# Hybrid decoder step on one core: filler doses, out-projection weights in a chain, two tiles by halves, maxima 0.75 of a head ahead

## The chip, the core and the metric

The kernel runs on one NeuronCore of a Trainium2 chip. The core has five engines with a queue of instructions each: TensorE (PE, matmuls, with its weight loads as PEld), VectorE (DVE), ScalarE (ACT), GpSimd (POOL) and SyncE (SP), which here does nothing but issue DMA transfers. The metric is the device time of one execution in microseconds, the median of several runs.

## The reference

One step of a decoder layer, on a prompt of 2048 positions and on one new position for each of 8 samples. What matters here is the prompt:

```python
h = rms_norm(x, g_norm)
q, k, v, fz, za, u, gv, zc = split(h @ w_in)             # 1024 -> 3592
q, k = rms_norm(q, g_q), rms_norm(k, g_k)                # 8 heads of 64
c = cumsum(log_sigmoid(fz + b_f))                        # per head, over positions
s[t, r] = q[t] . k[r] / 8 + c[t] - c[r]                  # only r <= t
attn = softmax(s) @ v
mix = tril(w_s) @ rms_norm(gv, g_v) + b_s                # in chunks of 128, 4 groups of 128 channels
y = x + concat(attn * silu(za), u * mix * silu(zc)) @ w_out      # 1024 -> 1024
```

The samples attend to 512 paged past positions as well, and also give their k, v, log f and normalised v rows.

## The kernel before, in words

The program has two phases. In the first, TensorE multiplies tiles of 128 positions, or blocks of 512, with the columns of `w_in`; a factor is split into a high and a low part, so that each product is three matmuls. q, k, v and the gates go to DRAM. For the second half of the positions (blocks `cp` 2 and 3) `za`, `u` and `zc` are not computed there: these products are left as *filler*.

The second phase is attention and out-projection. It goes over 32 *units* `(h, c)`, a head and a block of 512 queries, in the order of `UNITS`, which ends with (6,0), (6,1), (6,2), (7,0), (6,3), (7,1), (7,2), (7,3). In a unit (`values`) one step handles 128 keys: two matmuls into a bank `sc` (of three), an exponential on ACT into one of ten buffers `p`, a sum of these on POOL into `acc` (L1066, L1068), and, eight steps at a time, the products `av` of `p` and values. At the unit's end the result goes through ACT and VectorE (`at`), SP stores it (`aT`), and sums and row factors (`rT`) follow.

Into this stream, the order of TensorE's instructions is written by hand; `Pe.clock` is the program's own count of how much TensorE work has been given. Three things are put between the steps:

- *Maxima.* The exponential needs the maximum of each query's row. `maxima` computes scores in pieces into a bank `tp` (of three), which VectorE reduces (L993, L995); the results (`mrow`) are loaded with the queries of a unit by `load_queries` (tile `q2`). `AHEAD` says by how much of a head the maxima run ahead of the units. Their pieces for a head need the head's keys `k2`, whose loads (`load_head`, L906, and L909 for three rows `kx`) are asked for one by one, `LSTEP` apart, beginning in the second step of the unit (h-1, 0).
- *Filler.* `fill` gives as many of its steps (three matmuls into the bank `fl`) as a dose says: `FILL0` in units with c = 0, `FILL7` in the last three, else `FILL`, times the work of a step or piece. A job's weights `fh`, `fl` are asked for when the job before begins.
- *Work that waits for other engines*, given by `later` after so much of `Pe.clock`; `give` puts it into the engines' queues after the last matmul given. The other engines' queues are in the order that a scheduler found with these bounds; each queue is worked through in turn, and an instruction that waits holds up those behind it.

Out-projection (`out_tiles`) needs the 16 weight blocks `wo_hl` (8 blocks `k` of rows, two halves `f` of columns) and, by tile of 128 positions, `g` (attention and mixing, gated, from DRAM) and `xy`, the residual. A weight block is loaded into one of three buffers `raw` (L1137), cast by ACT and its remainder taken by VectorE (`split`, L268 and L273); an input likewise (`am`). The first tiles' inputs are there once the unit (7,0) has gone through its gate (`gate`, POOL's `gz`). After the last unit, `last_phase` runs what is left of 16 tiles.

Of the kernel before, what the change touches and what calls it, by code (L numbers as in the profile page):

```python
# [33 lines left out]
OQ, OK, OV, OF = 0, 512, 1024, 1536  # L34
OZA, OU, OGV, OZC = 1544, 2056, 2568, 3080
NCP = 2
FILL = 0.46
FILL0 = 0.9
FILL7 = 0.95
FLAG = 7000.0  # L40
WOLAG = 9000.0
WOSTEP = 1500.0
OLAG = 9000.0
GTLAG = 8000.0
STLAG = 5000.0
STLAST = 2500.0
SLAG = 4500.0
# [9 lines left out]
NTP = 3  # L57
NAV = 1
UNITS = [(h, c) for h in range(6) for c in range(4)] + [(6, 0), (6, 1), (6, 2), (7, 0), (6, 3), (7, 1), (7, 2), (7, 3)]
AHEAD = 0.65  # L60
LSTEP = 3000.0
LHEAD = 2500.0
VPARTS = 7
# [4 lines left out]
DGATE = 6000.0  # L68
OAHEAD = 3
KORDER = (4, 5, 6, 7, 0, 1, 2, 3)  # L70
WOENG = ('act',)
OFIRST = 2
PAIRS = (14,)
KSTART = 8
PACE = 800.0
# [11 lines left out]
def hymba_step(ctx, tc, x_prompt, x_sample, cache_k, cache_v, cache_logf, page_table, g_norm, w_in,  # L87
# [62 lines left out]
    def bank(tag, n=512):  # L150
        pool, bufs = pool_of[tag]
        return pool.tile([P, n], F32, tag=tag, bufs=bufs, name=tname(tag))


    class Pe:
# [2 lines left out]
        waiting = []  # L158
        given = 0
        loads, load_at = [], 0.0  # L160
        decode, side, steps = 1e12, 1e12, None
        last = None

# [3 lines left out]
    def later(ns, fn):  # L167
        Pe.given += 1
        Pe.waiting.append((Pe.clock + ns, Pe.given, fn))
        Pe.waiting.sort(key=lambda w_: w_[:2])  # L170

    def give():

        seen, last = len(nc.cur_bb.bb.instructions), Pe.last
        Pe.waiting.pop(0)[2]()
        for i in nc.cur_bb.bb.instructions[seen:] if last is not None else ():
            if i.engine != mybir.EngineType.PE:
                tc.add_manual_dep(i, last.name, mybir.DependencyInfo(mybir.DependencyClass.NoSync,
                                                                     mybir.DependencyReason.DATA), reason="given late")

    def pump(all_=False):
        while Pe.waiting and (all_ or Pe.waiting[0][0] <= Pe.clock):
            give()
        if not all_ and Pe.loads and Pe.clock >= Pe.load_at:
            load_next()
        if not all_ and Pe.clock >= Pe.side:
            m = next(mgen)
            mdone[0] += m
            Pe.side = Pe.clock + PACE if mdone[0] < AHEAD * MT else 1e12
        if not all_ and Pe.clock >= Pe.decode:  # L190
            Pe.decode = Pe.clock + (next(Pe.steps, None) or 1e12)

    def load_next():
        Pe.loads.pop(0)()
        Pe.load_at = Pe.clock + LSTEP

    def mm(out, lhsT, rhs, start, stop, ns):
        Pe.last = nc.tensor.matmul(out, lhsT, rhs, start=start, stop=stop).ins  # L198
        pe(ns)
# [65 lines left out]
    def split(hi, lo, src, eng):  # L265

        if eng == "act":
            nc.scalar.copy(hi, src)  # L268
        elif eng == "dve":
            nc.vector.tensor_copy(hi, src)  # L270
        else:
            nc.gpsimd.tensor_scalar(hi, src, 1.0, 0.0, op0=ALU.mult, op1=ALU.add)
        nc.vector.tensor_tensor(lo, src, hi.bitcast(F32), op=ALU.subtract)  # L273
# [566 lines left out]
    def filler():  # L840
        jobs = [(b, f) for f in range(4) for b in (8 + f, 4 * (f // 2) + f % 2, 4 * (f // 2) + 2 + f % 2)]
        nxt = first.pop()
        mxs = {}
        units = []
        for n, (o, f) in enumerate(jobs):
            units.append(nxt)
            if n + 1 < len(jobs):
                nxt = fill_weights(jobs[n + 1][0])
            if n + 2 >= len(jobs):
                continue  # L850
            unit = units.pop()
            while len(unit) < KT:
                yield -1
            for cp in range(NCP, 4):
                if n % 3 == 0:
                    yield from za_steps(unit, 0, f, cp, "fl")
                elif n % 3 == 1:
                    mxs[cp] = s2(t="mxu")
                    yield from u_steps(unit, 0, f, cp, "fl", mxs[cp])
                else:  # L860
                    yield from zc_steps(unit, 0, f, cp, "fl", mxs.pop(cp))
                yield 0
        while min(len(unit) for unit in units) < KT:
            yield -1
        for cp in range(NCP, 4):
            mx = s2(t="mxu")
            yield from u_steps(units[0], 0, f, cp, "fl", mx)
            yield 0
            yield from zc_steps(units[1], 0, f, cp, "fl", mx)
            if cp == 3:  # L870
                break
            yield 0
            while "all" not in heads.get(NH - 1, {}):
                yield -1
            load_out_weights(0)

    def fillers():
        yield from filler()
        load_out_weights(1)
        yield from out_tiles()  # L880

    fgen = fillers()
    debt, hold = [0.0], [0.0]

# [58 lines left out]

    def load_queries(h, c):
        while (h, c) not in shifted:
            if next(mgen, None) is None:
                give()
            pump()

        t = place("q2")  # L950
        a, cs = h * HD, slice(c * 512, (c + 1) * 512)
        for r in range(2):
            nc.sync.dma_start(t[r * HD:(r + 1) * HD, :512].bitcast(F32), qk_hi[a:a + HD, cs])
        nc.sync.dma_start(t[:HD, 512:].bitcast(F32), qk_lo[a:a + HD, cs])
        nc.sync.dma_start(t[HD + 2:HD + 3, 512:].bitcast(F32), mrow[h:h + 1, cs])
        return t
# [170 lines left out]
    def load_out_weights(f):  # L1127

        tiles = []

        def load(n, k):
            if n % 2 == 0:
                tiles.append(s8(F32R, "wo"))
            t = tiles[-1]
            hi, lo = (t[:, (2 * (n % 2) + r) * 512:(2 * (n % 2) + r + 1) * 512] for r in range(2))
            raw = raw2()
            nc.sync.dma_start(raw, wo[k * P:(k + 1) * P, f * 512:(f + 1) * 512])  # L1137

            def parts():
                split(hi, lo, raw, WOENG[n % len(WOENG)])  # L1140
                wo_hl[k, f] = hi, lo
            later(WOLAG, parts)
        for n, k in enumerate(KORDER):
            later(n * WOSTEP, lambda n=n, k=k: load(n, k))

    def gate(k, c):

# [20 lines left out]
    def out_inputs(i):  # L1168

        g, xy = s4(t="g"), s4(t="xy")  # L1170
        nc.sync.dma_start(g, gm[i].rearrange("p k t -> p (k t)"))
        nc.sync.dma_start(xy, x[i * P:(i + 1) * P])
        got = {}

        def parts():
            am = s8(F32R, "am")
            hi, lo = (am[:, r * D:(r + 1) * D] for r in range(2))
            split(hi, lo, g, "act")
            hi, lo = (t.rearrange("p (k t) -> p k t", k=KT) for t in (hi, lo))
            got.update(hi=hi, lo=lo, xy=xy)  # L1180
        later(OLAG, parts)
        return got

    def out_products(i, hi, lo, xy, tags):
        for f in range(2):
            fs = slice(f * 512, (f + 1) * 512)
            po = bank(tags[f])
            for n, k in enumerate(KORDER):
                wh, wl = wo_hl[k, f]
                mm(po, hi[:, k], wh, n == 0, False, 216)  # L1190
                mm(po, hi[:, k], wl, False, False, 216)
                mm(po, lo[:, k], wh, False, n == KT - 1, 216)
                yield 648
            nc.vector.tensor_tensor(xy[:, fs], xy[:, fs], po, op=ALU.add)  # L1194
            yield 0
            if i == NT - 1:
                nc.scalar.dma_start(y[i * P:(i + 1) * P, fs], xy[:, fs])
        if i < NT - 1:
            nc.scalar.dma_start(y[i * P:(i + 1) * P], xy)

    finished = [0]
# [2 lines left out]
    def prepare(i):  # L1204
        if i < NT and i not in ins and finished[0] > i // 4:
            ins[i] = out_inputs(i)
# [3 lines left out]
    def out_tiles():  # L1210

        gs = None
        for i in range(NT):
            while i not in ins or not ins[i] or len(wo_hl) < 2 * KT:
                prepare(i)
                if last_phase[0]:
                    give()
                else:
                    yield -1
            for n in range(1, OAHEAD + 1):  # L1220
                prepare(i + n)
            if i == 8:
                for _ in Pe.steps:
                    pass
                while decoded[0] < B:
                    give()
                gs = decode_out()
            if gs is not None and i < 12:
                next(gs, None)
            yield from out_products(i, **ins.pop(i), tags=("sc", "sc") if last_phase[0] else ("fl", "fl"))  # L1230

    mgen = all_maxima()
    mdone = [0.0]
# [185 lines left out]
```

## Time and profile before

| | us |
|---|---|
| median of 3 runs | 1329.95 |
| lowest, highest | 1324.32, 1331.84 |
| profiled execution: its time | 1327.27 |
| its span, first to last instruction | 1325.5 |
| start of unit (0,0) | 589.3 |
| start of unit (6,0), (6,2), (6,3) | 1010.5, 1029.0, 1066.0 |

The profile is of one execution. Its page gives busy time and share by engine, the span in 40 slices, and the costliest groups of instructions. A group's row reads: line, engine, operation, tiles written and read, shapes, count; then busy time, mean ns of one; then idle time of the engine before them and what ended it. Rows of a timeline read: start, length, engine, line, operation, count, and in brackets the idle time before and what ended it. A stretch's row gives busy time and record count of each engine, TensorE's granted clock (1.00 is full), DMA share and GB/s. A matmul record is one instruction of the hardware; the products `av` are two records each.

### The profile page before, as it was taken

Reading aid. Unit: us, or ns where it says so; the run is one execution under the profiler, and the core shown is the slowest. Engines: PE = TensorE matmul, PEld = TensorE weight load, DVE = VectorE, ACT = ScalarE, POOL = GpSimd, SP = SyncE. Lnnn points to the kernel's source line nnn. Section 1 sums busy time; section 2 is a strip of 40 time slices with the busy share of each in tenths; the row PEclk is TensorE's granted clock in tenths of the full one; section 3 lists DMA queues with packets and bytes.
Section 4 is the critical chain, followed back from the end, with each engine's and each line's share of the span. In section 5 each row is a group of like instructions: output and inputs, shape, how many; then the busy total and the mean of one; then the engine's idle time right before and its main releaser. Section 6 shows DMA issues by size and latency. Waiting matters only on the chain.

```text
span 1325.5 us, 19295 instructions
## 1 busy us (share of the span) xinstructions
PE 1294.4 (98%) x6544; PEld 1005.0 (76%) x6544; DVE 653.7 (49%) x1217; ACT 432.0 (33%) x781; POOL 559.9 (42%) x587
## 2 busy tenths in 40 slices
PE   6999999999999999999999999999999998999998
PEld 6999999999887877866666666666666564688877
DVE  5446664534678654254476544454455544422321
ACT  5542322222222111124444544344444356200100
POOL 3113343423232456215667565567567468600000
PEclk9999999999999999999999999999999898999999
DMA  7644353555213878946344856766474445573221
GB/s 218 197 122 106 88 144 112 151 144 149 73 43 83 291 240 261 310 112 157 81 129 132 221 137 164 205 175 174 131 204 118 112 131 173 184 265 118 96 81 48
DMA packets 189172, 201.43 MB, mean 152 GB/s; under 512 B 40018, under 2 KB 138642, under 8 KB 189050
## 3 DMA queue, kind: packets, MB, share of 16 engines
q1 hardware_dynamic: 185186, 191.43, 50.4%
q10 hardware_dynamic: 3488, 8.39, 1.7%
q8 instruction: 52, 0.85, 0.3%
q14 instruction: 46, 0.38, 0.1%
q0 software_dynamic: 400, 0.38, 0.1%
HBM read 127.43 MB, written 72.73 MB: 151 GB/s over the span
## 4 chain that ended last, share of the span: by engine, by line
PE 89%; DVE 3%; DMA 3%; issue 2%; ACT 1%; POOL 1%; SPq 1%; POOLq 0%; DVEq 0%; ACTq 0%
PE acc L198 35%; PE sc L198 23%; PE fl L198 10%; PE av L198 9%; PE tp L198 6%; PE tp L202 4%; PE pm L198 3%; POOL acc L1068 1%; DMA raw<-in_w_out_dram 1%; DVE mn L995 1%; DMA xp<-in_x_prompt_dram 0%; DMA wraw<-in_w_in_dram 0%; DVE mn L993 0%; DVE wl L281 0%; ACT p L1059 0%
## 5 line engine op out<-in xcount | busy, mean ns | idle before, releaser
L1068 POOL TENSOR_TENSOR acc<-acc,p 128x512 f32<-128x512 f32 (+3 forms) x256 | 289.4, 1131 | 78.7 <-ACT p L1059 63.1
L1059 ACT ACTIVATE p<-sc,zero 128x512 f32<-128x512 f32 (+1 forms) x320 | 194.0, 625 | 171.0 <-PE sc L198 162.6
L198 PE MATMUL acc<-wh,hh 128*128 128x384 f32 (+2 forms) x640 | 228.7, 357 | 0.8 <-ACT hh L268 0.8
L198 PE MATMUL acc<-wl,hh 128*128 128x384 f32 (+2 forms) x640 | 222.5, 348 | 1.0 <-DVE wl L281 1.0
L198 PE MATMUL acc<-wh,hl 128*128 128x384 f32 (+2 forms) x640 | 222.8, 348 | 0.7 <-DVE hl L273 0.6
L198 PE MATMUL sc<-q,k 128*128 128x512 f32 (+7 forms) x640 | 202.7, 398 | 6.7 <-ACT p L1059 6.6
L198 PE MATMUL sc<-wo,am 128*128 128x512 f32 x720 | 164.1, 390 | 0.0
L198 PEld LDWEIGHTS sc<-wo,am 128*128 128x128 f32 x720 | 134.9, 188 | 28.2
L995 DVE TENSOR_REDUCE mn<-tp 128x1 f32<-128x320 f32 (+5 forms) x192 | 118.9, 632 | 75.5 <-PE tp L198 74.6
L198 PEld LDWEIGHTS sc<-q,k 128*128 128x128 f32 (+1 forms) x640 | 119.1, 197 | 27.1 <-ACT p L1059 11.4
L198 PE MATMUL av<-p,vst 128*64 128x512 f32 (+3 forms) x640 | 137.2, 549 | 0.0
L198 PE MATMUL tp<-k,q 66*128 66x384 f32 (+6 forms) x320 | 122.3, 399 | 8.5 <-DMA k<-kx 1.7
L198 PEld LDWEIGHTS acc<-wh,hh 128*128 128x128 f32 x640 | 120.7, 189 | 8.2 <-ACT hh L268 1.5
L198 PEld LDWEIGHTS acc<-wh,hl 128*128 128x128 f32 x640 | 120.4, 188 | 6.8 <-DVE hl L273 1.6
L198 PEld LDWEIGHTS acc<-wl,hh 128*128 128x128 f32 x640 | 120.8, 189 | 5.9 <-DVE wl L281 1.4
L261 POOL TENSOR_SCALAR sm<-sm 128x6 f32<-128x6 f32 (+3 forms) x84 | 20.3, 242 | 243.4 <-DVE sm L447 169.9
L198 PEld LDWEIGHTS av<-p,vst 128*64 128x64 f32 x640 | 48.8, 139 | 68.2 <-issue 58.6
L993 DVE TENSOR_REDUCE mn<-tp 128x1 f32<-128x512 f32 (+7 forms) x128 | 66.8, 563 | 53.2 <-PE tp L198 52.7
L262 POOL TENSOR_TENSOR sm<-sm,mhalf 128x6 f32<-128x6 f32 (+3 forms) x84 | 89.0, 1060 | 6.7
L198 PEld LDWEIGHTS tp<-k,q 66*128 66x128 f32 x320 | 60.6, 191 | 37.6 <-DVE mn L995 6.2
L1066 POOL TENSOR_TENSOR acc<-p 128x512 f32<-128x512 f32 x32 | 41.1, 1284 | 110.4 <-ACT p L1059 98.9
L1194 DVE TENSOR_TENSOR xy<-xy,sc 128x512 f32<-128x512 f32 x30 | 20.6, 687 | 120.1 <-PE sc L198 120.1
(213 smaller groups left out, 1902.3 us busy)
## 6 DMA issues: line engine op xcount, KB each, us to landing
kb<-in_cache_k_dram SPq DMA_DIRECT2D x32, 256.0 KB
k<-qk_hi SPq DMA_DIRECT2D x32, 256.0 KB
q<-qk_hi SPq DMA_DIRECT2D x64, 128.0 KB
vb<-in_cache_v_dram SPq DMA_DIRECT2D x32, 256.0 KB
g<-gm SPq DMA_DIRECT2D x16, 512.0 KB
xy<-in_x_prompt_dram SPq DMA_DIRECT2D x16, 512.0 KB
out_dram<-xy ACTq DMA_DIRECT2D x15, 512.0 KB
qk_hi<-qkh SPq DMA_DIRECT2D x32, 192.0 KB
```

The lines of the kernel that those rows point to most:

```text
L198: Pe.last = nc.tensor.matmul(out, lhsT, rhs, start=start, stop=stop).ins
L202: Pe.last = nc.tensor.transpose(out, in_, idn).ins
L261: nc.gpsimd.tensor_scalar(r, ss, inv_n, EPS, op0=ALU.mult, op1=ALU.add)
L262: nc.gpsimd.tensor_tensor(r, r, mhalf[:rows, :n], op=ALU.pow)
L993: nc.vector.tensor_reduce(part[:, j_ % 4, n_:n_ + 1], sp, axis=AX.X, op=ALU.min)
L995: nc.vector.tensor_reduce(part[:, j % 4, n:n + 1], sp, axis=AX.X, op=ALU.min)
L1059: nc.scalar.activation(p[:, n0:], sp[:, n0:], AF.Exp, bias=zero1, scale=-1.0)
L1066: nc.gpsimd.tensor_tensor(acc, p0, p, op=ALU.add)
L1068: nc.gpsimd.tensor_tensor(acc[:, n0:], acc[:, n0:], p[:, n0:], op=ALU.add)
L1194: nc.vector.tensor_tensor(xy[:, fs], xy[:, fs], po, op=ALU.add)
```

## The change

It changes numbers and the places where three things are asked for.

1. `AHEAD` goes from 0.65 to 0.75, and maxima drawn by `load_queries` are counted in `mdone`.
2. The doses go from 0.46, 0.9, 0.95 to 0.42, 0.85, 0.6 (`FILL`, `FILL0`, `FILL7`).
3. The filler no longer stops until the last head's loads are all given, and no longer asks for out-projection's weights itself: it puts their half into `wo_due`, and `pump` asks for it once the last head is loaded. Of a half's eight blocks three are asked for at once, and each further one when the cast of the block three before it is given, 8 us of `Pe.clock` after its load instead of 9.
4. Out-projection goes over half tiles: (0, first half), (1, first), (0, second), (1, second), then the others as before. A half tile waits only for its own half of the weights. Inputs of tile 2 are asked for at the half tile before it, those of tiles 3 to 5 at its start.

```diff
-FILL = 0.46
-FILL0 = 0.9
-FILL7 = 0.95
+FILL = 0.42
+FILL0 = 0.85
+FILL7 = 0.6
-WOLAG = 9000.0
+WOLAG = 8000.0
-AHEAD = 0.65
+AHEAD = 0.75
...
         if not all_ and Pe.loads and Pe.clock >= Pe.load_at:
             load_next()
+        if Pe.wanted:
+            Pe.wanted()
...
             yield 0
-            while "all" not in heads.get(NH - 1, {}):
-                yield -1
-            load_out_weights(0)
+            wo_due.append(0)
 
     def fillers():
         yield from filler()
-        load_out_weights(1)
+        wo_due.append(1)
         yield from out_tiles()
 
+    wo_due = []
+
+    def wanted():
+        if wo_due and "all" in heads.get(NH - 1, {}):
+            load_out_weights(wo_due.pop(0))
+    Pe.wanted = wanted
...
         while (h, c) not in shifted:
-            if next(mgen, None) is None:
+            m = next(mgen, None)
+            if m is None:
                 give()
+            else:
+                mdone[0] += m
             pump()
...
             def parts():
-                split(hi, lo, raw, WOENG[n % len(WOENG)])
+                split(hi, lo, raw, "act")
                 wo_hl[k, f] = hi, lo
+                if n + 3 < KT:
+                    load(n + 3, KORDER[n + 3])
             later(WOLAG, parts)
-        for n, k in enumerate(KORDER):
-            later(n * WOSTEP, lambda n=n, k=k: load(n, k))
+        for n in range(3):
+            later(n * WOSTEP, lambda n=n: load(n, KORDER[n]))
...
-        for i in range(NT):
-            while i not in ins or not ins[i] or len(wo_hl) < 2 * KT:
+        halves = [(i, f) for f in range(2) for i in range(NHALF)] + [(i, f) for i in range(NHALF, NT) for f in range(2)]
+        for n, (i, f) in enumerate(halves):
+            while i not in ins or not ins[i] or (KORDER[-1], f) not in wo_hl:
...
-            for n in range(1, OAHEAD + 1):
-                prepare(i + n)
+            for j in range(min(NHALF, n + 2) if n < NHALF else i + 1, n - NHALF + 2 if n < 2 * NHALF else i + OAHEAD + 1):
+                prepare(j)
```

TensorE's instructions number the same on both sides; their order differs from the end of the first phase on. Numbers behind a tile's name tell its uses apart. In unit (6,2) before, TensorE's queue: `tp<-k2,q1` are maxima of head 7, `maskb` their mask.

```order
L198 MATMUL tp_1960_10895<-maskb_91,identb_84 128x128
L198 MATMUL tp_1961_10901<-k2_1897_10642,q1_999_6032 128x512
L198 MATMUL tp_1962_10904<-k2_1897_10642,q1_999_6032 128x512
L198 MATMUL tp_1963_10907<-k2_1897_10642,q1_999_6032 128x512
L198 MATMUL tp_1964_10910<-k2_1897_10642,q1_999_6032 128x512
L198 MATMUL tp_1965_10913<-k2_1897_10642,q1_999_6032 128x384
L198 MATMUL tp_1966_10915<-k2_1897_10642,q1_999_6032 128x512
L198 LDWEIGHTS identb_84
L198 MATMUL tp_1965_10913<-maskb_91,identb_84 128x128
L198 LDWEIGHTS identb_84
```

After, in the same unit: `fl` is filler, `sc` are scores of the unit.

```order
L202 MATMUL fl_1957_10873<-hh_95_634,fl_1879_10509 128x512
L206 MATMUL tp_1958_10883<-ident_79,sm_1946_10827 4x128
L206 MATMUL tp_1959_10886<-ident_79,mx_1947_10831 4x128
L202 MATMUL tp_1960_10892<-k2_1902_10620,q1_999_6032 128x512
L202 MATMUL sc_1961_10895<-q2_1030_6174,k1_1793_10076 128x512
L202 LDWEIGHTS identb_84
L202 MATMUL sc_1961_10895<-maskb_91,identb_84 128x128
L202 MATMUL sc_1961_10895<-q2_1030_6174,k2_1758_9925 128x512
L202 MATMUL tp_1962_10901<-k2_1902_10620,q1_999_6032 128x512
L202 MATMUL sc_1963_10904<-q2_1030_6174,k1_1793_10076 128x384
L202 LDWEIGHTS identb_84
L202 MATMUL sc_1963_10904<-maskb_91,identb_84 128x128
```

Six maxima pieces follow each other in the first, and each stands between scores or filler in the second.

SyncE's queue at the load of head 7's three key rows `kx`, before; ahead of it are queries of a unit, the result `at` of unit (6,0), and a product of the filler, `mxu`:

```order
L1082 DMA aT_119<-at_1884_10571 64x512
L906 DMA k2_1897_10642<-qk_hi_113 64x1024
L953 DMA q2_1030_6174<-qk_hi_113 64x512 x2
L954 DMA q2_1030_6174<-qk_lo_114 64x512
L955 DMA q2_1030_6174<-mrow_126 1x512
L1082 DMA aT_119<-at_1896_10635 64x512
L572 DMA gm_117<-mxu_1837_10332 128x4x128
L909 DMA k2_1897_10642<-kx_120 3x2048
L906 DMA k2_1897_10642<-qk_hi_113 64x1024
```

And after:

```order
L566 DMA mxu_1897_10607<-mixT_116 128x512
L1163 DMA gz_1900_10614<-zT_118 128x512
L1164 DMA ga_1899_10613<-aT_119 128x512
L1166 DMA gr_1901_10615<-rT_121 64x512 x2
L914 DMA k2_1902_10620<-qk_hi_113 64x1024
L1093 DMA aT_119<-at_1884_10538 64x512
L1174 DMA gm_117<-ga_1857_10428 128x4x128
L1093 DMA aT_119<-at_1893_10588 64x512
L917 DMA k2_1902_10620<-kx_120 3x2048
L914 DMA k2_1902_10620<-qk_hi_113 64x1024
```

The load of `kx` stands right behind the store of the result of unit (6,0) now, and the filler's product is not among the rows ahead of it.

ACT's queue in units (7,2) and (7,3), before: `p<-sc` are exponentials, `wo<-raw` casts of weights, `am<-g` of inputs, `at<-av` copies of results.

```order
L1059 ACTIVATE p_1021_6158<-sc_2088_11489,zero1_75 128x256
L1059 ACTIVATE p_1021_6158<-sc_2089_11495,zero1_75 128x128
L268 CAST wo_2061_11385<-raw_2062_11386 128x512
L1080 COPY at_2090_11505<-av_2079_11448 64x512
L268 CAST wo_2061_11385<-raw_2063_11388 128x512
L1059 ACTIVATE p_1022_6159<-sc_2091_11515,zero1_75 128x512
L1059 ACTIVATE p_1022_6159<-sc_2092_11519,zero1_75 128x512
L268 CAST wo_2066_11399<-raw_2067_11400 128x512
L268 CAST am_2094_11531<-g_2072_11425 128x1024
L268 CAST am_2095_11534<-g_2074_11429 128x1024
L1059 ACTIVATE p_1022_6159<-sc_2093_11524,zero1_75 128x512
L1059 ACTIVATE p_1022_6159<-sc_2096_11537,zero1_75 128x512
```

After, in unit (7,2):

```order
L1070 ACTIVATE p_1022_6159<-sc_2067_11403,zero1_75 128x512
L1070 ACTIVATE p_1022_6159<-sc_2068_11408,zero1_75 128x512
L1070 ACTIVATE p_1022_6159<-sc_2069_11413,zero1_75 128x512
L1070 ACTIVATE p_1022_6159<-sc_2071_11420,zero1_75 128x512
L1070 ACTIVATE p_1023_6160<-sc_2072_11427,zero1_75 128x512
L1070 ACTIVATE p_1023_6160<-sc_2073_11432,zero1_75 128x512
L272 CAST am_2077_11450<-g_2050_11334 128x1024
L272 CAST am_2078_11453<-g_2052_11338 128x1024
L272 CAST wo_2065_11400<-raw_2066_11401 128x512
L1070 ACTIVATE p_1021_6158<-sc_2081_11468,zero1_75 128x512
```

The casts of the two inputs stand behind the eighth exponential of unit (7,2) now, where they stood in unit (7,3) among the weights' casts.

More of the change, by code (lines that the diff above doesn't have):

```diff
@@ L44 @@
 GTLAG = 8000.0
+OLAG0 = 9000.0
 STLAG = 5000.0
@@ L70 @@
 KORDER = (4, 5, 6, 7, 0, 1, 2, 3)
-WOENG = ('act',)
 OFIRST = 2
+NHALF = 2
 PAIRS = (14,)
@@ L160, in hymba_step @@
         loads, load_at = [], 0.0
+        wanted = None
         decode, side, steps = 1e12, 1e12, None
@@ L1180, in parts, with out_products @@
             got.update(hi=hi, lo=lo, xy=xy)
-        later(OLAG, parts)
+        later(OLAG if i >= OFIRST else OLAG0, parts)
         return got
[L1184 to L1198, printed above, removed]
+    def out_products(i, f, hi, lo, xy, tag):
+        fs = slice(f * 512, (f + 1) * 512)
+        po = bank(tag)
+        for n, k in enumerate(KORDER):
+            wh, wl = wo_hl[k, f]
+            mm(po, hi[:, k], wh, n == 0, False, 216)
+            mm(po, hi[:, k], wl, False, False, 216)
+            mm(po, lo[:, k], wh, False, n == KT - 1, 216)
+            yield 648
+        nc.vector.tensor_tensor(xy[:, fs], xy[:, fs], po, op=ALU.add)
+        yield 0
+        if i == NT - 1:
+            nc.scalar.dma_start(y[i * P:(i + 1) * P, fs], xy[:, fs])
+        elif f == 1:
             nc.scalar.dma_start(y[i * P:(i + 1) * P], xy)
@@ L1212, in out_tiles @@
         gs = None
-        for i in range(NT):
-            while i not in ins or not ins[i] or len(wo_hl) < 2 * KT:
+        halves = [(i, f) for f in range(2) for i in range(NHALF)] + [(i, f) for i in range(NHALF, NT) for f in range(2)]
+        for n, (i, f) in enumerate(halves):
+            while i not in ins or not ins[i] or (KORDER[-1], f) not in wo_hl:
                 prepare(i)
                 if last_phase[0]:
+                    pump()
                     give()
@@ L1219, in out_tiles @@
                     yield -1
-            for n in range(1, OAHEAD + 1):
-                prepare(i + n)
-            if i == 8:
+            for j in range(min(NHALF, n + 2) if n < NHALF else i + 1, n - NHALF + 2 if n < 2 * NHALF else i + OAHEAD + 1):
+                prepare(j)
+            if (i, f) == (8, 0):
                 for _ in Pe.steps:
@@ L1227, in out_tiles @@
                 gs = decode_out()
-            if gs is not None and i < 12:
+            if gs is not None and i < 12 and f == 0:
                 next(gs, None)
-            yield from out_products(i, **ins.pop(i), tags=("sc", "sc") if last_phase[0] else ("fl", "fl"))
+            yield from out_products(i, f, **ins[i], tag="sc" if last_phase[0] else "fl")
     mgen = all_maxima()
```

## The prediction

> **What bounds the kernel now.** I read the page first, then the waits of TensorE, then tables of stretches, then the timelines of the worst stretches.
>
> The page's first part and two lines of its second: share of busy time by engine, and tenths of busy time and of granted clock in 40 slices of 33 us.
>
> ```profile
> PE 1294.4 (98%) x6544; PEld 1005.0 (76%) x6544; DVE 653.7 (49%) x1217; ACT 432.0 (33%) x781; POOL 559.9 (42%) x587
> PE   6999999999999999999999999999999998999998
> PEclk9999999999999999999999999999999898999999
> ```
>
> TensorE is the bound nearly everywhere. But a matmul counts as busy while it is slow, and between slices 31 and 35, the end of attention, the clock is not full. So I count matmul records per microsecond. The columns are the length, then busy time and records (x) of each engine, then granted clock and DMA share:
>
> ```profile
> 589.30:982.10 392.80, 388.95 (x1978) 252.49 (x1977) 201.09 (x360) 177.66 (x320) 245.27 (x222) 1.00 0.58 157
> 1010.50:1029.00 18.50, 16.79 (x93) 11.08 (x92) 10.51 (x19) 8.92 (x16) 12.03 (x11) 1.00 0.62 170
> 1029.00:1058.10 29.10, 26.99 (x104) 14.70 (x103) 18.13 (x35) 9.64 (x19) 14.18 (x14) 0.82 0.38 103
> 1066.00:1155.40 89.40, 82.81 (x364) 51.10 (x363) 42.50 (x50) 47.45 (x85) 67.76 (x52) 0.92 0.50 157
> 1155.40:1325.50 170.10, 166.21 (x737) 134.61 (x735) 43.80 (x53) 13.70 (x15) 1.28 (x1) 0.99 0.35 125
> ```
>
> In 24 even units of attention a record takes 392.80 / 1978 = 0.199 us. The stretch of unit (6,2), 1029.0 to 1058.1, has 104 records, worth 20.7 us, and takes 29.1: **8.4 us lost**. From unit (6,3) to the first tiles of the out-projection, 1066.0 to 1155.4, 364 records are worth 72.3 us and take 89.4: **17.1 us lost**. Unit (6,1) before them loses nothing by this measure (93 x 0.199 = 18.5). From 1155.4 on TensorE runs out-projection without a break. So 25.5 us are what this change can reach at the end.
>
> Why they are lost, first in unit (6,2). TensorE's timeline, and the reductions that empty its banks:
>
> ```profile
> 1042.83 2.46 PE L198 MATMUL tp<-k,q 66*128 66x512 f32 x5
> 1045.45 0.50 PE L198 MATMUL tp<-k,q 66*128 66x512 f32 x1 [0.15 <-DVE mn L995]
> ...
> L995 DVE TENSOR_REDUCE mn<-tp 128x1 f32<-128x512 f32 (+3 forms) x13 | 7.7, 630 | 4.7 <-PE tp L198 4.6
> ```
>
> Maxima pieces come in a row there. Each is emptied by VectorE in 0.630 us, three times what a record takes, and there are three banks: TensorE goes at VectorE's pace, and then its clock is halved (below).
>
> Second, after 1066. Waits of TensorE from 982 to 1155.4 (total, times, longest), ACT's timeline around the longest, and from the chain of waits the load that ACT waited for:
>
> ```profile
> PE sc L198 <- ACT p L1059: 6.6, 3, 3.4
> PE tp L198 <- DMA k<-kx: 1.7, 1, 1.7
> ...
> 1113.70 0.59 ACT L1080 COPY at<-av 64x512 f32<-64x512 f32 x1 [0.47 <-PE av L198]
> 1117.27 0.62 ACT L268 CAST wo<-raw 128x512 fp32r<-128x512 f32 x1 [2.98 <-DMA raw<-in_w_out_dram]
> 1117.91 1.26 ACT L1059 ACTIVATE p<-sc,zero 128x512 f32<-128x512 f32 x2
> 1119.07 0.62 ACT L268 CAST wo<-raw 128x512 fp32r<-128x512 f32 x1
> 1119.58 2.00 ACT L268 CAST am<-g 128x1024 fp32r<-128x1024 f32 x2
> ...
> 1109.46 7.79 DMA raw<-in_w_out_dram
> ```
>
> The cast of an out-projection weight stands in ACT's queue ahead of the exponentials that scores wait for. Its load took 7.79 us, ACT stood for 2.98, and TensorE with it. The clock follows:
>
> ```profile
> 1047.20:1057.50 10.30, 9.78 (x30) 5.85 (x30) 5.75 (x12) 2.36 (x5) 3.44 (x4) 0.50 0.24 68
> 1081.40:1084.80 3.40, 1.72 (x8) 1.09 (x7) 0.69 (x1) 2.95 (x7) 0.98 (x1) 1.00 0.12 18
> 1084.80:1088.20 3.40, 3.40 (x11) 2.27 (x10) 0.00 (x0) 1.89 (x4) 3.17 (x4) 0.50 0.70 215
> 1118.90:1129.20 10.30, 8.82 (x21) 3.63 (x22) 9.00 (x6) 8.16 (x14) 9.79 (x7) 0.50 0.61 206
> ```
>
> After each wait TensorE has half its clock for 3.4 or 10.3 us. In the two windows after 1066 that is 13.7 us at 0.50, worth 6.9 us. So the 17.1 are 6.6 of waits for ACT, 6.9 of clock, and 3.6 of small ones.
>
> **The change part by part.** No instruction is added or removed: 6192 matmuls of the program on both sides, and the same casts, loads and stores. Everything is order.
>
> *Maxima 0.75 of a head ahead, and those drawn by `load_queries` counted.* In unit (6,2) before, queries of (7,0) are asked for before their maxima are ready, which empties the generator: 17 pieces with nothing else between. In the new order no more than three stand together anywhere in attention; the four blocks of (6,2) are spread between scores. I take 8 of the 8.4 us; bounds 5 (another wait takes some of it) and 8.4.
>
> *The price of it: keys of the next head.* Maxima of a head begin sooner after its keys are asked for. SyncE's queue takes things in turn, so the load `kx` (rows of the gate, needed by the first piece) leaves behind what stands ahead of it. Before, for head 7, by the chain of waits:
>
> ```profile
> 1017.59 0.69 ACT th L547
> 1018.30 0.70 DVE sz L548
> 1019.07 1.29 POOL mxu L571
> 1020.38 0.38 SPq L572
> 1020.80 3.03 DMA k<-kx
> 1023.97 0.60 PE tp L198 x4
> ```
>
> The filler's last result of a job went through three engines and a store ahead of `kx`, 6.2 us to its landing at 1023.83; that is the 1.7 us wait. Counted in the order, between the last TensorE work that `kx` stands behind and the piece that reads it there were 96, 89, 87, 90, 94, 53 and 25 records for heads 1 to 7; now 42, 43, 32, 39, 36, 19 and 18, or 8.4, 8.6, 6.4, 7.8, 7.2, 3.8 and 3.6 us. What has to fit: for head 7 now the copy of a result (0.59 on ACT), its sum on VectorE, a store's issue, and 3.03 of landing, with VectorE and the issue at:
>
> ```profile
> 1114.93 0.67 DVE L1081 TENSOR_TENSOR at<-at,av 64x512 f32<-64x512 f32 x1
> 1018.05 0.46 SPq L1082 DMA_DIRECT2D aT<-at  x1
> ```
>
> So 0.59 + 0.67 + 0.46 + 3.03, with some 0.3 between, 5.1 us: late by 1.5. Head 6 stands behind a copy on ACT and four stores of the decode, which I set between that 5.1 and the 6.2 above: late by 1.3 to 2.4, say 2. Heads 1 to 5 fit, head 3 just. Together 3.5 us, less the 1.7 that go: **+2** with rounding. Bounds: 0 (SyncE runs ahead) and seven heads late by a whole landing, 7 x 3.03 - 1.7 = 19.5.
>
> *Weights apart from the filler, in a chain of three, 8 us from load to cast.* The next load now leaves when a buffer's cast has been given, so none stands in SyncE's queue waiting for a buffer ahead of queries and stores. In the new order at least 31 records, 6.2 us, lie between the TensorE work that a load waits for and the one that ACT waits for ahead of its cast; before, eight of the 16 weights had 19 or fewer, two of them none. The row above has 7.79 us at the worst, with 512 KB loads beside it. So casts wait 1 us at one or two places instead of 2.98 and more.
>
> *Filler at 0.42/0.85/0.6 instead of 0.46/0.9/0.95.* Same matmuls, given more evenly. Unit (6,0) starts at matmul 4904 of the program instead of 4936, so 32 (6.4 us) are left for the end, and the filler no longer stops until head 7 has all its keys: before, units (6,1) and (6,2) have none and (6,3) 27, now 15, 24 and 33. POOL, which sums the exponentials, must keep up in units (7,1) and (7,2). POOL's row for one burst, eight sums:
>
> ```profile
> 1083.82 9.11 POOL L1068 TENSOR_TENSOR acc<-acc,p 128x512 f32<-128x512 f32 x8 [4.01 <-ACT p L1059]
> 1119.26 1.28 POOL L1066 TENSOR_TENSOR acc<-p 128x512 f32<-128x512 f32 x1 [1.78 <-ACT p L1059]
> ```
>
> At 9.11 / 8 = 1.14 a sum, units (7,1) and (7,2), 18 sums with two products at 1.28, are 23 us of POOL, beside 124 records of the new order, 24.7 us. POOL is nearly level there, and ten buffers of exponentials, 11 us of sums, lie between it and TensorE; I allow 1 us.
>
> *First two tiles by halves.* The first matmul of out-projection now needs only the first half of the weights, and comes in unit (7,2) instead of (7,3); the second half is needed two half tiles, 48 matmuls, later. The casts of the first inputs (2.00 us above) fall under eight value products. Tile 2's input is asked for only 24 matmuls ahead, 5.5 us at 170.1 / 737 = 0.231, and must land and be cast:
>
> ```profile
> 1104.19 2.76 DMA gm<-ga
> L268 ACT CAST am<-g 128x1024 fp32r<-128x1024 f32 x12 | 12.6, 1051 | 86.6 <-DVE xy L1194 78.9 <-DMA g<-gm 7.2 <-DVE amTs L273 0.4
> L273 DVE TENSOR_TENSOR am<-g,am 128x1024 fp32r<-128x1024 f32 x12 | 14.6, 1218 | 0.0
> ```
>
> With 2.76 to 7.79 of landing plus 1.05 and 1.22 that is 5.0 to 10.1, but its load stands right behind the last result's store in SyncE's queue and leaves some 10 us ahead of its use. Between 0 and 4.6, I take **+0.5**.
>
> Of the 17.1 us, then, 4 stay (1 at casts, 1 at POOL, 2 of small waits): **-13**. Bounds -5 (the filler's 32 matmuls fill idle time, and every wait on ACT stays) and -17.1.
>
> Sum: -8 + 2 - 13 + 0.5 = -18.5; for units 0 to 23, whose filler shifts a little, I add 1 (bounds -2 and 3): **-17.5 us**. The profiled execution took 1327.27 (span 1325.5) and would take 1309.8. The median of the runs shown is 1329.95, 2.7 above it, so 1312.5 by the median; I say 1312.
>
> What a late key costs beyond itself hangs on the clock. In 1081.4 to 1084.8 TensorE was busy for 1.72 of 3.40 us, and the next 3.4 were at 0.50; so a wait of 1.7 us can cost another 1.7, and head 6 or 7 might add that. [...]
>
> **The rivals.**
> - *Late keys at three heads or more, with a halved window or two*: 3.03 at three more heads, 5.2 for a window of 10.3: +14, 1326. For it: every lead was cut to half or less. Against it: five of seven still fit.
> - *ACT still blocks at the end*: only -5 of the 17.1, so 1320. For it: 16 casts still share ACT with exponentials, and out-projection's loads meet 512 KB inputs. Against it: loads leave 6.2 us ahead or more.
> - *The doses do nothing*: the filler ends in unit (7,1) in both orders, so the end has no more cover, and only the maxima gain: 1329.95 - 6 = 1324. Against it: out-projection's first matmuls now stand in (7,2).
> - *Slower*: all seven heads late by a landing, each followed by 3.4 us at half clock: 7 x (3.03 + 1.7) = 33 in place of the 2, 1343. It decides from about 2.8 us a head. Against it: SyncE would have to lag by more than any of its rows above.
>
> **How the numbers follow.** 0.5%, 6.65 us, is about what a measurement of this kernel can tell from no change; the line is at 1323.3. Chances: forecast 0.62 (1303 to 1319), ACT 0.14, late keys 0.11, doses 0.07, slower 0.06. Faster: 0.62 + 0.14 and a third of the next two, 0.81. Slower by over 0.5%: 0.06. The rest 0.13. The range reaches from all 25.5 us regained and 3 more (1301) to the late keys' 1326.
>
> **What would show it.** Right: no stretch of maxima in a row in unit (6,2), and it takes some 20 us; granted clock 1.00 from 1020 to 1150; waits of scores for ACT under 2 us; the wait for `kx` at 3 to 4 us, at heads 6 and 7; a first out-projection matmul in (7,2). Wrong: waits for `kx` at most heads, casts still held by `raw`, a gap ahead of tile 2, or halved windows anywhere.

## The result: 0.5% slower, 1336.24 us

The changed kernel takes 1336.24 us (median of 5 runs, 1332.08 to 1338.53), the kernel before 1329.95 (1324.32 to 1331.84): a ratio of 1.005, 95% interval 1.0029 to 1.0072. The forecast was 1312, in a range of 1301 to 1326. The profiled execution took 1336.24, with a span of 1334.4.

The page of the changed kernel, the same three lines as before:

```profile
PE 1294.7 (97%) x6544; PEld 1009.9 (76%) x6544; DVE 652.6 (49%) x1217; ACT 433.9 (33%) x781; POOL 558.8 (42%) x587
PE   6999999999999999999999998989998899999998
PEclk9999999999999999999999999989999899999999
```

TensorE's instructions number the same, and its busy time is the same to 0.3 us. Counted from 0, the nines of its row are broken from slice 24 on, where before they held to slice 32. Waits of TensorE in the 32 units (total, times, longest):

```profile
PE tp L202 <- DMA k<-kx: 15.8, 3, 7.1
PE tp L202 <- DVE mn L1004: 2.7, 4, 1.9
...
PE sc L202 <- ACT p L1070: 0.9, 1, 0.9
```

The waits for ACT went from 6.6 us to 0.9, as forecast. Those for the key rows `kx` went from 1.7 to 15.8. Stretches of the changed kernel: units (0,0) to (5,2) (the prediction's row of these has 23 units too, not 24); (6,1); (6,2); (6,3) to the first tiles of out-projection. Then the three halved windows that follow the waits:

```profile
592.98:998.87 405.89, 391.07 (x1959) 252.83 (x1958) 201.12 (x361) 178.86 (x321) 244.80 (x222) 0.98 0.56 148
1026.55:1052.43 25.88, 18.77 (x80) 13.01 (x80) 7.85 (x16) 6.21 (x12) 9.65 (x11) 0.74 0.47 128
1052.43:1072.59 20.16, 20.15 (x99) 13.07 (x99) 10.25 (x20) 9.58 (x18) 14.25 (x13) 1.00 0.51 139
1079.14:1163.40 84.26, 83.26 (x392) 53.60 (x391) 48.03 (x60) 46.95 (x84) 67.86 (x53) 0.98 0.50 149
...
818.30:821.70 3.40, 3.40 (x12) 2.23 (x11) 0.62 (x2) 0.80 (x2) 1.95 (x2) 0.50 0.96 221
893.40:900.20 6.80, 6.38 (x23) 4.78 (x23) 2.47 (x5) 1.57 (x4) 2.27 (x2) 0.50 0.18 50
1033.40:1047.00 13.60, 9.37 (x30) 6.96 (x30) 3.05 (x7) 1.63 (x3) 2.53 (x2) 0.50 0.40 104
```

Unit (6,2), 29.1 us before, takes 20.16, and 392 records in 84.26 us lose 84.26 - 392 x 0.199 = 6.3 where 17.1 were lost. Both gains are there. But units (0,0) to (5,2) take 405.89 us for 1959 records, where 392.80 did for 1978, and unit (6,1) 25.88 for 80, worth 15.9. The three windows are 23.8 us at half clock, worth 11.9; with the 15.8 of waits that is **27.7 us for late keys**, where the forecast has 2. Two more halved windows of 3.4 us, at 712.5 and 1122.1, follow other waits, of 1.94 us for VectorE and 0.88 us for ACT.

For all kernels below I made one account: each TensorE instruction at the median spacing of its form in the profile before, summed in the kernel's order, and taken from the measured start times. It gives what TensorE loses in each stage of the profiled execution (us):

| | before (0,0) | (0,0) to (5,2) | (5,3) to (6,1) | (6,2), (7,0) | (6,3) to the end | sum |
|---|---|---|---|---|---|---|
| before | 20.6 | 20.1 | 3.7 | 11.2 | 16.2 | 71.9 |
| changed | 22.7 | 37.9 | 13.6 | 0.8 | 5.9 | 80.8 |
| changed, keys early (below) | 23.9 | 23.4 | 2.6 | 0.8 | 4.4 | 55.1 |

80.8 - 71.9 = 8.9 is the difference of the two profiled executions, 1336.24 - 1327.27. The first column varies by 3.3 us between kernels whose first phase is alike; what moves it stays open.

Where the late load stood. In the changed kernel, the last TensorE work that head 7's `kx` stands behind, SyncE's queue from there to `kx`, then from the chain its landing, and TensorE's wait:

```profile
1025.11 1.50 PE L202 MATMUL av<-p,vst 128*64 128x512 f32 x8
...
1025.03 1.09 SPq L964 DMA_DIRECT2D q<-qk_hi  x2
1026.21 0.55 SPq L965 DMA_DIRECT2D q<-qk_lo  x1
1026.81 0.42 SPq L966 DMA_DIRECT2D q<-mrow  x1
1027.32 0.36 SPq L566 DMA_DIRECT2D mxu<-mixT  x1
1027.73 0.42 SPq L1163 DMA_DIRECT2D gz<-zT  x1
1028.21 0.42 SPq L1164 DMA_DIRECT2D ga<-aT  x1
1028.67 1.09 SPq L1166 DMA_DIRECT2D gr<-rT  x2
1029.80 0.59 SPq L914 DMA_DIRECT2D k<-qk_hi  x1
1030.49 0.54 SPq L1093 DMA_DIRECT2D aT<-at  x1
1031.08 0.59 SPq L1174 DMA_DIRECT2D gm<-ga  x1
1031.77 0.56 SPq L1093 DMA_DIRECT2D aT<-at  x1
1032.37 0.58 SPq L917 DMA_DIRECT2D k<-kx  x1
...
1032.37 5.07 DMA k<-kx
...
1037.58 0.77 PE L202 MATMUL tp<-k,q 66*128 66x128 f32 x2 [7.05 <-DMA k<-kx]
```

SyncE issues one transfer after another, 13 in 7.3 us, with no gap of more than 0.1. The last product in the first row began at 1026.2; TensorE wanted the keys at 1030.5 (1037.58 less 7.05), 1.8 us before they were even asked for. I call *lag* the time from the start of the last TensorE instruction that `kx` stands behind to its issue: 9.35 us at head 4, 10.52 at head 5, 6.14 at head 7. The landings took 2.2, 3.2 and 5.1:

```profile
807.96 0.38 SPq L576 DMA_DIRECT2D gm<-mxu  x1
...
814.43 2.23 DMA k<-kx
...
890.58 3.15 DMA k<-kx
```

Not all of the two longer lags is issuing. At head 4 SyncE first stood 2.9 us for a product of the filler (the first row), and at head 5 some 2.6 us of waits lie between its issues.

The profile before had the same thing, hidden under a longer *lead* (the time from the end of that TensorE work to the first piece that reads the keys). Its rows at head 3, of which the prediction showed none, SyncE's between two of TensorE:

```profile
732.47 1.50 PE L198 MATMUL av<-p,vst 128*64 128x512 f32 x8
...
732.76 1.09 SPq L953 DMA_DIRECT2D q<-qk_hi  x2
733.90 0.58 SPq L1150 DMA_DIRECT2D gz<-zT  x1
...
738.30 1.85 SPq L562 DMA_DIRECT2D mxu<-mixT  x1
740.19 0.47 SPq L1082 DMA_DIRECT2D aT<-at  x1
740.70 0.59 SPq L906 DMA_DIRECT2D k<-qk_hi  x1
741.40 0.54 SPq L1082 DMA_DIRECT2D aT<-at  x1
741.98 0.46 SPq L909 DMA_DIRECT2D k<-kx  x1
...
750.93 0.40 PE L198 MATMUL tp<-k,q 66*128 66x128 f32 x2
```

The last product ahead of it began at 733.6, so it lagged by 8.4 us; the first piece came at 750.9, 9 us after the issue, and nobody waited. With the change's lead of 6.2 us there, such a lag is a wait.

### The profile page after: what moved, and what is told of

Same layout as the page of the kernel before. It is cut to its first block, busy times and chain, and to the rows that moved or that the text cites. A ratio compares the mean times of both kernels' runs of the same rounds, so it can differ in the third digit from the quotient of the medians.

```text
span 1334.4 us, 19317 instructions
## 1 busy us (share of the span) xinstructions
PE 1294.7 (97%) x6544; PEld 1009.9 (76%) x6544; DVE 652.6 (49%) x1217; ACT 433.9 (33%) x781; POOL 558.8 (42%) x587
## 4 chain that ended last, share of the span: by engine, by line
PE 93%; DVE 3%; DMA 2%; ACT 1%; issue 1%; SPq 1%; POOL 0%; DVEq 0%; ACTq 0%; POOLq 0%
PE acc L202 36%; PE sc L202 23%; PE fl L202 11%; PE av L202 10%; PE tp L202 6%; PE tp L206 4%; PE pm L202 3%; DMA k<-kx 1%; DMA gr<-rT 1%; DVE mn L1006 0%; DMA wraw<-in_w_in_dram 0%; DVE mn L1004 0%; DVE wl L285 0%; DMA gT<-in_g_norm_dram 0%; DMA kb<-in_cache_k_dram 0%
## 5 line engine op out<-in xcount | busy, mean ns | idle before, releaser
L202 PE MATMUL tp<-k,q 66*128 66x384 f32 (+6 forms) x320 | 122.1, 394 | 22.6 <-DMA k<-kx 15.8
L202 PEld LDWEIGHTS tp<-k,q 66*128 66x128 f32 x320 | 61.7, 194 | 48.5 <-issue 20.1
L202 PE MATMUL acc<-hh,wh 128*128 128x512 f32 x192 | 75.1, 391 | 0.0
```

## The experiments

Theory: the gain is as forecast, and early maxima outrun `kx`, which SyncE's queue delays. Rival: the lower doses, with less filler between scores, expose TensorE in units (0,0) to (6,1).

**Keys early.** The decisive one, since TensorE's order stays the same instruction for instruction:

```diff
-LHEAD = 2500.0
+LHEAD = 0.0
...
-        return [lambda: keys(0), rows_of, lambda: keys(1)], [
+        return [lambda: (keys(0), rows_of()), lambda: keys(1)], [
```

> The changed kernel, whose kx and first half of keys are asked for together at the second step of the unit (h-1, 0) instead of 2.5 and 5.5 us of TensorE work later; TensorE's order is the same instruction for instruction. Theory keys: leads of kx grow to 23.0, 17.4, 14.6, 15.5, 11.3, 16.1 and 11.0 us; with lags up to 10.5 and a landing of 3 to 5 only heads 5 and 7 can still be late, by 0 to 3: waits for k under 4 us, no halved clock at the heads: 1336 - 25 = 1311 (1306 to 1317). Theory doses: 1336, within 4. If SyncE's queue as a whole is the bound (the earlier request only waits longer): waits stay near 15 us, 1336.

Measured: 1310.43 us (1309.38 to 1310.88), ratio to before 0.9856 (0.9834 to 0.9879). No wait for keys is left: `kx` left 8.0 to 14.2 us before TensorE wanted it at heads 1 to 7. The clock of the page, the longest waits, and units (0,0) to (5,2), (6,1) of this kernel:

```profile
PEclk9999999999999999999999999999999999999999
PE tp L202 <- DVE mn L1004: 2.7, 4, 2.0
PE tp L202 <- DVE mn L1006: 1.3, 3, 0.8
...
594.24:985.62 391.38, 385.88 (x1960) 249.98 (x1958) 201.10 (x361) 178.91 (x321) 245.23 (x222) 1.00 0.57 155
1013.30:1028.19 14.89, 14.32 (x80) 10.07 (x80) 7.84 (x16) 6.22 (x12) 9.70 (x11) 1.00 0.79 221
```

405.89 became 391.38 and 25.88 became 14.89, with the same work. So the late keys cost 25.8 us (1336.24 less 1310.43), near the 27.7 counted above, and the rest of the change gains what was forecast. This version beats both kernels. A nine of the clock's row can hide 3.4 us at half clock: one such window, at 713.7, is left here, and it follows no wait for keys.

**`kx` from another queue.** Asked for at the same place of the program, TensorE's order the same:

```diff
-            nc.sync.dma_start(hd["k2"][HD:HD + 3].bitcast(F32), kx[h])
+            nc.scalar.dma_start(hd["k2"][HD:HD + 3].bitcast(F32), kx[h])
```

> The changed kernel with the three rows kx loaded from ACT's queue instead of SyncE's, asked for at the same point of the program; TensorE's order is the same, and so are SyncE's other loads and their leads (12.3, 14.2, 11.4, 12.3, 11.3, 12.9 and 5.3 us for the first half of the keys, heads 1 to 7). Theory queue (kx was late because SyncE worked through what stood ahead of it): no wait for k at heads 1 to 6; at head 7 the first half of the keys, on SyncE, is now the last to come, late by 6.1 + 3 - 5.3 = 4: 1310.4 + 5 to 8 = 1317 (1311 to 1321). Theory landing (the transfer of three rows itself is slow here, or it is asked for too late whatever the queue): waits for kx near 15 us stay, 1336.

Measured: 1321.84 us (1320.47 to 1325.51), ratio 0.9943 (0.9925 to 0.9962), 0.8 above the range. Waits of TensorE, and the two rows behind the first line, with the landings from the chain:

```profile
PE tp L202 <- DMA k<-qk_hi: 9.0, 2, 5.3
...
885.64 0.77 PE L202 MATMUL tp<-k,q 66*128 66x128 f32 x2 [3.74 <-DMA k<-qk_hi]
1026.98 0.77 PE L202 MATMUL tp<-k,q 66*128 66x128 f32 x2 [5.29 <-DMA k<-qk_hi]
...
878.62 6.88 DMA k<-qk_hi
1020.98 5.87 DMA k<-qk_hi
```

No wait for `kx` is left. On ACT's queue head 7's load left at 986.24, 35 us before TensorE wanted it; on SyncE's it left at 1032.37, 1.8 us after. So neither its data nor its buffer held it there: its 15.8 us were its place in SyncE's queue and what stood ahead. Since the load also left so much sooner, this run does not part a busy queue from a late place in it. Next to come was a second load, the first half of the keys, still on SyncE: late at head 7 as expected, and at head 5 too, where its landing took 6.88. Asking for `kx` from ACT's queue gains 14 us (1336.24 - 1321.84), asking earlier 26.

**One late load priced.** Keys early for heads 1 to 6; head 7's two loads apart and as late as in the changed kernel. Of the edit's two places, the time of asking (the other keeps `keys(0)` and `rows_of` apart for head 7 alone):

```diff
-                Pe.load_at = Pe.clock + LHEAD
+                Pe.load_at = Pe.clock + (LHEAD if h + 1 == NH - 1 else 0.0)
```

> The kernel with keys early for heads 1 to 6; head 7's asked for as in the changed kernel. TensorE's order stays. It prices one late load: lead 3.7 us as there, so a wait near 7.05 us and 13.65 us at half clock behind it. Theory A (what a wait costs is the wait and half of the halved window): 1310.4 + 7.0 + 6.8 = 1324 (1318 to 1326). Theory B (the halved clock is partly absorbed by later waits): 1317.

Measured: 1318.86 us (1314.4 to 1322.29), ratio 0.9916 (0.989 to 0.9941): 8.4 us more than with all keys early. The wait was 6.1 us, nearly that of the changed kernel, but the clock was halved for 6.8 us behind it, not 13.65:

```profile
PE tp L202 <- DMA k<-kx: 6.1, 1, 6.1
```

By theory A's rule (the wait and half of the halved window) the bill is 6.1 + 3.4 = 9.5; 8.4 was paid, 1.1 less, so the rule held here to within that, and the length of the halved window was the wrong guess.

**`AHEAD` 0.75 alone**, in the kernel before:

```diff
-AHEAD = 0.65
+AHEAD = 0.75
```

> The kernel before with AHEAD at 0.75 alone. Theory keys: leads of kx fall to 9.8, 9.7, 9.9, 7.8, 6.7, 5.4 and 2.3 us for heads 1 to 7, while SyncE's lags in the profile before were 2.9, 2.4, 8.4, 2.4, 5.3, 2.8 and 3.7 and a landing takes 3: heads 3, 5, 6 and 7 are late by 1.5, 1.6, 0.4 and 4.4, about 8 us, with as much again in halved clock; the block of maxima in unit (6,2) goes (8.4) and the old wait of 1.7. 1330 + 16 - 10 = 1336 (1330 to 1343), waits for kx 6 to 14 us. Theory doses: the doses are the old ones, so only the gain of the block is left: 1330 - 8 = 1322.

Measured: 1333.07 us (1331.22 to 1335.59), ratio 1.0027 (1.0013 to 1.0042).

```profile
PE tp L198 <- DMA k<-kx: 6.6, 3, 4.0
PE sc L198 <- DMA q<-qk_hi: 5.1, 1, 5.1
```

The account has 0.6 us in (6,2) and (7,0) instead of 11.2, and 7.4 and 8.8 more in the two stages ahead of them. The keys were late here too, with the old doses, at heads 3, 6 and 7. The same with the two edits of early keys:

> The kernel before with AHEAD 0.75 and keys early and together, nothing else of the change. Theory A: the maxima's gain with its price taken away, 1330.2 - 8.4 (block of unit (6,2)) - 1.7 (old wait for kx) = 1320 (1317 to 1324); and against AHEAD 0.75 alone (1333.07) 13 us less, for 6.6 of waits for kx and some 7 of halved clock. Theory B (queries and exponentials wait instead, as the 5.1 for q in the run with AHEAD alone): 1326 to 1330.

Measured: 1318.98 us (1316.98 to 1321.0), ratio 0.9915 (0.9893 to 0.9937), 14 us below `AHEAD` alone. Early maxima and early keys together gain 11 us on the kernel before; early keys without early maxima were not run.

**`AHEAD` 0.65 in the changed kernel:**

```diff
-AHEAD = 0.75
+AHEAD = 0.65
```

> The changed kernel with AHEAD back at 0.65, all else of the change kept. Theory keys (the early maxima outrun the load kx, which SyncE issues up to 10.5 us after the TensorE work it stands behind; three waits of 15.8 us and 11.9 us of halved clock behind them): by the order, kx has leads of 18.9, 16.2, 17.9, 16.6, 13.9, 8.0 and 5.3 us for heads 1 to 7, so no wait at heads 1 to 6 and up to 2 us at head 7; 27 us come back. But a block of 21 maxima records in a row now stands in the middle of attention, as one stood in unit (6,2) before, worth some 8 us: 1336 - 27 + 8 = 1317 (1311 to 1322). Theory doses (less filler per unit exposes TensorE in units 0 to 25): the doses are kept, so 1336, within 5. The unit block: if maxima in a row cost nothing by themselves, 1309.

Measured: 1323.95 us (1319.41 to 1328.56), ratio 0.9957 (0.9939 to 0.9975), 2 above the range. The doses' rival would have 1336. Keys are late only at head 7 (2.5 us, with 6.8 us at half clock behind). But blocks of maxima are in other units now, in (0,2) for one; two stretches there:

```profile
624.80:628.20 3.40, 2.98 (x9) 1.54 (x8) 3.34 (x8) 0.00 (x0) 0.00 (x0) 0.77 0.21 74
628.20:631.60 3.40, 3.39 (x9) 1.77 (x8) 3.12 (x8) 0.00 (x0) 0.00 (x0) 0.50 0.73 182
```

In the first, nine records stand where 17 would; VectorE is busy nearly throughout, and the clock is halved: unit (6,2)'s trouble elsewhere. Units (0,0) to (5,2) lose 36.7 us, 13 more than with keys early, where I had set 8.

**The doses.** The changed kernel with 0.46, 0.9 and 0.95 again, with late keys and then with early ones:

```diff
-FILL = 0.42
-FILL0 = 0.85
-FILL7 = 0.6
+FILL = 0.46
+FILL0 = 0.9
+FILL7 = 0.95
```

> The changed kernel with the old doses (0.46, 0.9, 0.95). Theory keys: leads of kx are 9.8, 9.7, 9.9, 7.8, 6.7, 5.4 and 2.3 us, no better at heads 4 to 7, so waits for kx of 8 to 18 us stay, and the end has less cover: 1330 to 1345. Theory doses (the lower doses cost units 0 to 25 their 27 us): 1336 - 27 = 1309, with some 5 lost again at the end: 1309 to 1316.

> The kernel with keys asked for early and together (1310.43) with the old doses, 0.46, 0.9, 0.95. Theory A (the doses pay only at the end of attention, by the work left for units (6,3) to (7,1)): no wait for kx (leads 12.0 to 23.7 us), the filler ends in unit (7,0), units (6,3) to (7,3) have none: some 10 us lost there again, 1320 (1315 to 1324). Worked out from the run with the old doses and late keys: 1331.5 less its 5.7 of waits for kx and 6.8 of halved clock behind them, 1319. Theory B (the doses are worth nothing either way): 1310, within 3.

Measured: 1331.5 us (1326.49 to 1337.21), ratio 1.0012 (0.9995 to 1.0029); and 1317.16 (1314.76 to 1320.78), ratio 0.9906 (0.9883 to 0.9929). The first fells the rival, which would have 1309. What it does gain comes with keys that are less late, at heads 3 and 7 here:

```profile
PE tp L202 <- DMA k<-kx: 5.7, 2, 4.0
```

In the second the account has 21.4 us in units (0,0) to (5,2), against 23.4 with the new doses, and 16.2 from (6,3) on, against 4.4: the doses cost 2 early and save 12 late.

**The doses without the rest.** The kernel before with `AHEAD` 0.75, early keys and the new doses (the last fence read backwards), nothing else:

> The kernel before with three things alone: AHEAD 0.75, keys early and together, the new doses 0.42, 0.85, 0.6. Weights of out-projection still asked for by the filler and 1.5 us apart, no half tiles, nothing counted by the queries. TensorE's order is that of the kernel with keys early up to unit (7,2), where it has no first products of out-projection. Theory A (the doses alone bring the end's gain, 318.98 to 1310): 1310 (1307 to 1313). Theory B (doses, asking apart and half tiles each bring some of it): casts ahead of exponentials in (7,3) still cost 5 to 8 us, 1315 to 1319.

Measured: 1317.08 us (1314.48 to 1317.29), ratio 0.9911 (0.9892 to 0.993). Theory B has the time: from (6,3) on 12.4 us are lost, 7.4 to the end of attention and 5.0 in out-projection. Its reason is not borne out: scores waited 2.2 us for ACT, against 0.9 in the kernel with keys early, and another 2.5 us were waits for POOL's sums; the rest of the loss stays open. Neither the doses nor the rest alone (16.2) does it; both together leave 4.4.

**No chain of weights**, and **whole tiles**, each in the kernel with early keys; the first edit is the fence, the second `NHALF = 0` for 2:

```diff
-                if n + 3 < KT:
-                    load(n + 3, KORDER[n + 3])
...
-        for n in range(3):
-            later(n * WOSTEP, lambda n=n: load(n, KORDER[n]))
+        for n, k in enumerate(KORDER):
+            later(n * WOSTEP, lambda n=n, k=k: load(n, k))
```

> The kernel with keys early (1310.43), the weights of out-projection asked for 1.5 us apart as before, not in a chain; TensorE's order stays. Theory A (the chain keeps ACT free at the end): loads stand in SyncE's queue for a buffer again and casts ahead of exponentials: scores wait 4 to 7 us for ACT, as much again in halved clock, 1320 (1314 to 1325). Theory B (asking apart from the filler is what counts, the chain adds nothing): 1310, within 3.

> The kernel with keys early (1310.43) with whole tiles in out-projection (NHALF = 0); TensorE's order is the same up to the first 9 products of out-projection in unit (7,2), after which the second half of tile 0 needs the second half of the weights 24 matmuls on instead of 48. Theory A (halves matter, the second half of the weights would hold TensorE at the end of attention): 3 to 10 us lost there, 1313 to 1320. Theory B (weights are there in time either way): 1310, within 3.

Measured: 1308.68 us (1306.92 to 1310.01), ratio 0.9837 (0.9814 to 0.986) without the chain: my theory fell, the chain adds nothing that shows. With whole tiles 1313.37 (1310.5 to 1313.84), ratio 0.9884 (0.9864 to 0.9904). The intervals of it and of the kernel with half tiles overlap; the account has 7.8 us from (6,3) on against 4.4, so half tiles may save some 3 us, which stays unsettled.

## Why the prediction was wrong

The step that failed is "the price of it: keys of the next head", **+2, bounds 0 and 19.5**. By the runs it is 25.8 (1336.24 - 1310.43): the loads left late because of what stood ahead of them in SyncE's queue, and behind the three waits the clock was halved for 3.41, 6.83 and 13.65 us.

- The leads were counted rightly: 6.2 to 9.1 us at heads 1 to 5, from the end of the TensorE work (the lags count from its start, some 0.3 us before). What they were set against was not. "What has to fit" took head 7's chain, 5.1 to 6.2 us, for every head: the path of data through ACT, VectorE and one store. It left out the other issues in SyncE's queue. The lags were 9.35 and 10.52 us at heads 4 and 5, to the issue alone, without the landing.
- The bound was no bound: "seven heads late by a whole landing" supposes that the load is issued when its data are ready. Three heads were late, by 3.4, 5.3 and 7.05 us, each by more than the 3.03 of that landing.
- "SyncE would have to lag by more than any of its rows above" was true of the rows quoted, and two rows not quoted, 8.4 at head 3 and 5.25 at head 5, would have said otherwise. 8.4 + 3.03 of landing against a lead of 6.2 is 5 us late at head 3, where I wrote "fit, head 3 just". Head 3 in fact lagged by only 2.7 in the changed kernel, and heads 4 and 5 had the long lags: a lag belongs to a burst of issues, not to a head. With `AHEAD` alone heads 3, 6 and 7 were late.
- Halved clock was "might add" and in no term; it was 11.9 of the 27.7.

The rival "late keys at three heads or more" had the waits, the halved clock and the number of heads, and about half the price (+14); the cause, SyncE's lag, stood only in the rival "slower", as what it would need. The rival "ACT still blocks at the end" fell with its waits, 0.9 us; "the doses do nothing" fell with the 12 us above.

The other terms, by the account (changed against before):

- Maxima: -8 forecast, -10.4 in (6,2) and (7,0). Right in mechanism, 2.4 more in size. `AHEAD` alone does it.
- Weights, doses and the end: -13 forecast, with 4 staying; -10.3 by the account, 5.9 staying. Right in the main. Its reason was half wrong: not the chain, but the doses together with weights asked for apart from the filler, and perhaps half tiles. By the experiments no part alone gives the sum.
- Units 0 to 23: +1 forecast, 2 to 3.3 by the runs with early keys.
- Tile 2 by halves: +0.5 forecast; no gap showed, and half tiles may gain 3.

With the key term at zero the sum was -19.5, 1310.5 by the median; the kernel with early keys takes 1310.43. That they meet within 0.1 us is luck. The terms above miss by 1 to 3 us in both directions, the first phase lost 3.3 us more in that profile, which no term held, and the profiled execution before was 2.7 us below its median. The prediction's "24 even units" are 23.

## What to carry to other kernels

When work is moved earlier, take the lag at every place where the load occurs, not only where it is late now: a queue's lag that nobody waits for today is in the profile as the distance between an issue and the work it depends on. Count the issues that stand ahead, at some 0.5 us each (13 took 7.3 us at head 7), beside the path of the data. Then move the request by as much as the reader: here two lines turned 0.5% lost into 1.4% gained.

## What the runs showed of the hardware that I had not expected

- Issuing has a price: ahead of head 7's `kx` SyncE took 0.36 to 0.59 us an issue, 13 of them without a gap of more than 0.1 us. Single issues were longer, 1.85 us at head 3 before.
- By the clock records of the two profiles, windows at a granted clock of 0.50 in attention lasted 10.24, 3.41 and 10.24 us before, and 3.41 (three times), 6.83 and 13.65 in the changed kernel. The same wait did not give the same length: 4.0 us for head 7's keys was followed by 13.65 us with `AHEAD` alone and by 6.83 in the changed kernel with the old doses. Short waits had half clock behind them too: one of 2.5 us (`AHEAD` 0.65, head 7) 6.8 us, and in the changed kernel one of 0.88 us, with TensorE busy for 2.52 of the 3.40 us up to 1122.1, 3.41 us.
- The landing of the same three rows took 2.23, 3.15 and 5.07 us at heads 4, 5 and 7 of the changed kernel, that of half the keys 6.88 and 5.87 with `kx` from ACT's queue.
